# Hybrid decoder block on one core: sums of squares of queries by four products in column groups of TensorE, and the norms of row blocks in one chain

## The chip, the cores and the metric

One NeuronCore of a Trainium2 chip runs the whole kernel in one launch. The metric is the time on the device in microseconds, the median over runs. Engines are named as in the profile: PE is TensorE's matmul unit and PEld its weight load, DVE is VectorE, ACT ScalarE, POOL GpSimd, SP SyncE, whose queue issues every transfer of this kernel.

## The reference

For x of 1024 rows and 1024 columns (float32) the layer computes two branches from one projection, merges them, and adds an MLP:

```python
h = rms_norm(x, norm_mix_g); proj = h @ w_in
gq, gk, gv = split(silu(causal_short_conv(g_qkv, conv_w)))          # 8 heads of 128
gq = l2_normalize(gq) * 128 ** -0.5; gk = l2_normalize(gk)
o_gdn = rms_norm(gated_delta_rule_chunked(gq, gk, gv, g, beta), gdn_norm_g) * silu(z)
o_att = dsa_sparse_attention(a_q, a_k, a_v, i_q, i_k, i_w)          # top 256 keys per query
x = x + (sigmoid(gate_a) * o_gdn + sigmoid(gate_b) * o_att) @ w_out
h2 = rms_norm(x, norm_mlp_g)
x = x + square(relu(h2 @ w_mlp_up)) @ w_mlp_down
```

l2_normalize divides a query by the root of its sum of squares plus 1e-6, and rms_norm of the second kind divides a row of the new x by the root of the mean of its squares. The change is about these two sums.

## The kernel before

The kernel is one stream of instructions per engine, whose order is fixed when it is built. The order comes from a planner, the class Weave (L2092): each piece of work is a generator with a priority (a smaller number goes first), which yields when it wants others to have a turn, when it waits for a named event, or, by yielding "A", "V" or "G", until that engine is free. Weave keeps a clock, prices each instruction by simple formulas (L2202 to L2223), and always takes the ready generator of the best priority. On the chip each engine then runs its list strictly in that order and waits on semaphores.

The stages, in the order of time: input norm and first projections (to about 250 us); the gated-delta branch, head after head, beside dense products of 512 columns with weights in a high and a low part (gdense, to about 940); sparse attention in 16 steps (8 blocks of 128 rows, in the order 0, 7, 1, 6, 2, 3, 5, 4, and two groups of heads; values_out turns the softmax rows pr into pt on PE) with the output projection; from about 1140 the MLP, whose two products are computed by a scheme of seven products of halves, so that sums and differences of row blocks (t1 to t4) are turned, rounded to a high and a low part, and multiplied.

*Queries.* conv (L774) makes q of a head as 128 channels by 1024 positions. queries (L1015) first calls squares (L918): PE transposes the eight blocks of q into two banks of the ring tt, and ACT squares each block with an accumulated sum over the channels, which gives qss, one number per position with positions on partitions. Then come the products of keys and queries. The only reader of qss is output (L1114), after the scan of the head.

*Norms of row blocks.* residual (L1413) adds the output projection to a block x1, stores it to XD, and has ACT sum its squares into nss. roots (L1439) turns such sums into reciprocal roots nr by 11 small DVE operations. norm2 (L1448) is started when the attention is nearly over: roots of blocks 0, 1 and 2, then of 3, scaling of both halves of each block (DVE the first, ACT the second), transposes, and rounding in norm_out. early (L1481), once for blocks 6 and 7 and once for block 5, takes roots, scales the second half on ACT, and forms sums and differences; early_columns (L1499) turns them and early_rounded (L1525, priority 2) rounds them, ACT the high part hh and DVE the low part hl, and frees the bank. norm2b (L1677, priority -1) does the same for block 4, the last; its last_columns (L1704) needs a bank of the ring ss. Behind the event ("T", 2, 3) it subtracts t4[j] -= t2[j] for all four blocks in one go.

Of the kernel before, what the change touches and what calls it, by code (L numbers as in the profile page):

```python
# [9 lines left out]
F32 = mybir.dt.float32  # L10
F32R = mybir.dt.float32r
BF16 = mybir.dt.bfloat16
# [14 lines left out]
H = 8  # L27
# [23 lines left out]
def body(tc, a, out, dbg=None):  # L51
# [26 lines left out]


    padl, padl_es = pool("padl", side="left")  # L80
    G.memset(padl.tile([P, 32], F32, name="padl"), 0.0)
    cst, cst_es = pool("cst", side="left")
    dr, dr_es = pool("dr", space=DRAM)
    htp, ht_es = pool("htp", side="left")
# [110 lines left out]
    def after(key):  # L195
        wv.add(0, later(wv.busy["SY"] + SY_LATENCY, key))
# [478 lines left out]

    M1 = [dr.tile([4, P, S], F32, name=f"M1_{g}") for g in range(2)]
    SG = [dr.tile([4, P, S], F32, name=f"SG_{g}") for g in range(2)]
    ZA = [dr.tile([NB, 4, 32, 32], F32, name=f"ZA{h}") for h in range(H)]
    ZU = [dr.tile([NB * 4, 8, 4, 32], F32, name=f"ZU{h}") for h in range(H)]

# [93 lines left out]
    def conv(u):  # L774
        h, c = gunits[u]
        ct = ctile[c] + h
        yield ("gp",)
        if len(convs) > 1:
            yield ("conv", convs[-2])
        convs.append(u)  # L780
        cu = gq.tile([P, 3 + S], F32, name="cu", bufs=2)
        G_.memset(cu[:, 0:3], 0.0)
        for half in range(2):
            yield ("half", (u, half))
            wv.add(-1, cdrain(cu, u, half))
# [12 lines left out]
        yield  # L798
        o = (gq if c == "v" else gp).tile([P, S], F32, name={"k": "kt", "q": "qt", "v": "t4"}[c],
                                          bufs={"k": 3, "q": 2, "v": 1}[c])  # L800
        A_.activation(o, cu[:, 0:S], AF.Copy, scale=cw[0])
        for j in range(1, 4):
            yield
            yield "V"
            V_.scalar_tensor_tensor(o, cu[:, j:j + S], cw[j], o, op0=OP.mult, op1=OP.add)
        yield
        yield "A"
        A_.activation(cu[:, 0:S], o, AF.Tanh, scale=0.5)
        yield
        yield "V"  # L810
        V_.scalar_tensor_tensor(o, cu[:, 0:S], 1.0, o, op0=OP.add, op1=OP.mult)
        yield
        st[h][c + "t"] = o
        wv.done("conv", u)
        wv.add(2, {"k": keys, "q": queries, "v": values}[c](h))

# [98 lines left out]
        wv.add(1, join(h))  # L915


    def squares(t, ss):  # L918
        for half in range(2):
            yield tt.ready  # L920
            ps, slot_ = tt.get()
            for i in range(4):
                PE_.transpose(ps[:, i, :], blk(t, half * 4 + i), ident)
            yield
            for i in range(4):
                b = half * 4 + i
                junk = gp.tile([P, P], BF16, name="gj")
                A_.activation(junk, ps[:, i, :], AF.Square, accum_out=ss[:, b:b + 1])
                if i % 2:
                    yield  # L930
            tt.free(slot_)


    def decayed(h):
# [81 lines left out]
    def queries(h):  # L1016
        qt = st[h]["qt"]
        yield ("keys", h)
        if h > 1:
            yield ("out", h - 2)  # L1020
        kt, aq = st[h]["kt"], st[h]["aq"]
        qss = st[h]["qss"] = gp.tile([P, NB], F32, name="qss", bufs=3)
        yield from squares(qt, qss)
        for half in range(2):
            hs = slice(half * 4, half * 4 + 4)
            yield tt.ready
            ps, slot_ = tt.get()
# [85 lines left out]

    def output(h):  # L1114
        yield ("gate", (h, "a"))
        oss, qss, oo, og = (st[h][k] for k in ("oss", "qss", "vv", "kt"))
        fo = gp.tile([P, NB], F32, name="fo", bufs=2)
        fe = gp.tile([P, NB], F32, name="fe", bufs=2)
# [294 lines left out]
    def residual(qb, pw):  # L1413
        yield ("x", qb)
        yield 0.2
        for c in range(2):
            cs = slice(c * HALF, (c + 1) * HALF)
            V_.tensor_tensor(x1[qb][:, cs], x1[qb][:, cs], pw[c], op=OP.add)
        yield
        wv.done("x1", qb)  # L1420
        SY_.dma_start(XD[qb * P:(qb + 1) * P, :], x1[qb])
        after(("xd", qb))
        junk = tp.tile([P, D], BF16, name="th", bufs=2)
        A_.activation(junk, x1[qb], AF.Square, accum_out=nss[:, qb:qb + 1])
        yield
        wv.done("ss", qb)
# [9 lines left out]
        yield  # L1436
        wv.done("h2k", half, k)

    def roots(tbs):  # L1439
        for tb in tbs:  # L1440
            yield ("ss", tb)
        bs = slice(min(tbs), max(tbs) + 1)
        V_.tensor_scalar(nms[:, bs], nss[:, bs], 1.0 / D, EPS, op0=OP.mult, op1=OP.add)
        yield from rsq_w(cst, nr[:, bs], nms[:, bs], len(tbs), "n2", apart=False)
        yield


    def norm2():  # L1448
        tbs = [qb for qb, g in ATT if g and qb // 4 == first]
        for now in (tbs[:3], tbs[3:]):  # L1450
            yield from roots(now)
            for tb in now:
                yield ("xd", tb)
                for c, eng in enumerate("VA"):
                    yc = x1[tb][:, c * HALF:(c + 1) * HALF]
                    yield eng
                    if c:
                        A_.activation(yc, yc, AF.Copy, scale=nr[:, tb:tb + 1])
                    else:
                        V_.tensor_scalar(yc, yc, nr[:, tb:tb + 1], None, op0=OP.mult)  # L1460
        yield
        for c in range(2):
            ys = [x1[first * 4 + i][:, c * HALF:(c + 1) * HALF] for i in range(4)]
            for k in range(4 * c, 4 * c + 4):
# [13 lines left out]
    y22, comb, pairs = {}, {}, {}  # L1478
    places = {0: 0, 2: 2, 3: 4, 1: 6}

    def early(tbs):  # L1481
        yield from roots(tbs)
        for tb in tbs:
            i, r = tb % 4, nr[:, tb:tb + 1]
            b11, b12 = part(first, 0)[i], part(1 - first, 0)[i]
            y22[i] = part(1 - first, 1)[i]
            yield ("xd", tb)
            yield "A"
            A_.activation(y22[i], y22[i], AF.Copy, scale=r)
            yield  # L1490
            yield ("turned", 0)
            yield "V"
            V_.scalar_tensor_tensor(b11, b12, r, b11, op0=OP.mult, op1=OP.subtract)
            yield "V"
            V_.scalar_tensor_tensor(b12, b12, r, y22[i], op0=OP.mult, op1=OP.subtract)
            yield
            wv.done("combined", i)

    def early_columns():  # L1499
        js = [tb % 4 for tb in EARLIER]  # L1500
# [3 lines left out]
        for m in (0, 2):  # L1504
# [6 lines left out]
            for k in range(4):  # L1511
# [6 lines left out]
                ps, slot_ = ring.get()  # L1518
                for j in js:
                    PE_.transpose(ps[:, j * P:(j + 1) * P], y22[j][:, k * P:(k + 1) * P], ident)  # L1520
                wv.add(2, early_rounded(m, k, ps, ring, slot_))
        yield
        wv.done("early")

    def early_rounded(m, k, ps, ring, slot_):  # L1525
        cs = slice(min(EARLIER) % 4 * P, (max(EARLIER) % 4 + 1) * P)
# [25 lines left out]
    vl[1] = pA.tile([P, NB, P], F32R, name="vl1")  # L1552
    wv.add(1, vprep(1))
    wv.add(4, score())
    wv.add(0, loadm())
    wv.add(0, loadx())
    wv.add(1, wout_weights())
# [12 lines left out]

    wv.run(until=("pv", NA - 2))
    wv.add(8, norm2())
    for tbs in (EARLIER[1:], EARLIER[:1]):
        wv.add(2, early(tbs))
    wv.add(2, early_columns())


# [99 lines left out]
    def norm2b():  # L1677
# [15 lines left out]
        V_.scalar_tensor_tensor(t3[i], t3[i], r, y, op0=OP.mult, op1=OP.subtract)  # L1693
        yield ("T", 2, 3)
        wv.add(1, columns(3, t3))
        yield "V"
        for j in range(4):
            V_.tensor_tensor(t4[j], t4[j], t2[j], op=OP.subtract)
        yield ("col", 3)
        wv.add(1, columns(1, t1))  # L1700
        yield ("col", 1)
        wv.add(1, columns(4, t4))

    def last_columns(m, i, row):  # L1704
# [480 lines left out]
class _Ordered:  # L2185
# [12 lines left out]
    def __getattr__(self, op):  # L2198
# [3 lines left out]
        def call(*args, **kw):  # L2202
# [5 lines left out]
            if name == "PE":  # L2208
                fast = op == "matmul" and args[1].dtype == F32R
                if op == "matmul" and not fast and "tile_position" not in kw:  # L2210
                    return wv.issue(name, ins, (n * 1.67 + 5) / 1e3, 0.25)
                if op == "matmul" and "tile_position" in kw:
                    return wv.issue(name, ins, 0.03, 0.25)
                return wv.issue(name, ins, (n * (0.417 if fast else 0.835) + (13.4 if wv.shared else 2.5)) / 1e3, 0.25)
            if name == "SY":
                return wv.issue(name, ins, max(0.5, n * o.shape[0] / 9e4), SY_LATENCY)
            if name == "A":
                return wv.issue(name, ins, 0.13 + n / 1200 + (0.1 if "accum_out" in kw else 0), 0.15)
            if name == "V":
                return wv.issue(name, ins, 0.07 + n / 960, 0.12, self.port(op, args, kw))  # L2220
            if op == "tensor_tensor":
                return wv.issue(name, ins, 0.33 + n / 476, 0.2, True)
            return wv.issue(name, ins, 0.15 + n / 1000, 0.2)  # L2223
# [50 lines left out]
```

## Time and profile before

| | us |
|---|---|
| median of 3 runs | 1806.71 |
| lowest and highest run | 1806.06, 1808.27 |
| the profiled execution's own time | 1806.61 |
| its span, first to last instruction | 1804.9 |

The span is what the profile shows; the 1.7 us between it and the execution's own time lie around it. Durations are of instructions as the profiler records them; matmuls are pipelined, so that a row's start to the next row's start says more than its length. All operations are recorded by one helper, so every row has the same line, L2203, and tiles are told apart by their names: tt is the ring of banks for transposes of the gated-delta stage, dd the bank of dense products, jj that of the small products in tiles of the array, w a slot that holds weights or a row block, m a slot of the MLP.

### The profile page before, as it was taken

Reading aid. Unit: us, or ns where it says so; the run is one execution under the profiler, and the core shown is the slowest. Engines: PE = TensorE matmul, PEld = TensorE weight load, DVE = VectorE, ACT = ScalarE, POOL = GpSimd, SP = SyncE. Lnnn points to the kernel's source line nnn. Section 1 sums busy time; section 2 is a strip of 40 time slices with the busy share of each in tenths; the row PEclk is TensorE's granted clock in tenths of the full one; section 3 lists DMA queues with packets and bytes.
Section 4 is the critical chain, followed back from the end, with each engine's and each line's share of the span. In section 5 each row is a group of like instructions: output and inputs, shape, how many; then the busy total and the mean of one; then the engine's idle time right before and its main releaser. Section 6 shows DMA issues by size and latency. Waiting matters only on the chain.

```text
span 1804.9 us, 28444 instructions
## 1 busy us (share of the span) xinstructions
PE 1783.6 (99%) x10252; PEld 1517.6 (84%) x10252; DVE 1287.2 (71%) x2746; ACT 1022.8 (57%) x2186; POOL 533.3 (30%) x738
## 2 busy tenths in 40 slices
PE   9999999999999999999999999989999999999999
PEld 8999998888888888888888888768888888888887
DVE  5556768867877788875368677776766668969673
ACT  6566656656676554553457666666766664333331
POOL 0003530743362415753014121222323222222230
PEclk9999999999999999999999999999999999999999
DMA  5111242232222222232355221315445459473241
GB/s 165 50 47 47 71 129 65 50 97 77 66 64 71 53 65 69 75 86 75 95 186 183 76 90 53 114 38 184 167 152 170 135 185 363 133 250 122 100 136 52
DMA packets 192193, 198.80 MB, mean 110 GB/s; under 512 B 36738, under 2 KB 140467, under 8 KB 192051
## 3 DMA queue, kind: packets, MB, share of 16 engines
q1 hardware_dynamic: 192050, 196.97, 34.7%
q8 instruction: 81, 1.33, 0.3%
q14 instruction: 62, 0.50, 0.1%
HBM read 141.20 MB, written 55.74 MB: 109 GB/s over the span
## 4 chain that ended last, share of the span: by engine, by line
PE 93%; DVE 4%; ACT 1%; issue 1%; POOL 1%; DMA 0%; SPq 0%; ACTq 0%; POOLq 0%; DVEq 0%
PE dd L2203 55%; PE o L2203 15%; PE s L2203 7%; PE pt L2203 6%; PE tt L2203 3%; PE cc L2203 2%; PE sq L2203 2%; PE oo L2203 1%; PE jj L2203 1%; DVE w L2203 1%; DVE hl L2203 1%; DVE m L2203 0%; PE tp L2203 0%; DVE n2t L2203 0%; DMA pj<-in_x_dram 0%
## 5 line engine op out<-in xcount | busy, mean ns | idle before, releaser
L2203 PE MATMUL dd<-hh,w 128*128 128x512 f32 x1568 | 517.4, 401 | 0.0
L2203 PEld LDWEIGHTS dd<-hh,w 128*128 128x128 f32 x1568 | 289.0, 189 | 51.4
L2203 PE MATMUL dd<-hl,w 128*128 128x512 f32 x784 | 316.2, 403 | 0.9 <-DVE hl L2203 0.9
L2203 ACT ACTIVATE m<-m 128x512 f32<-128x512 f32 (+1 forms) x240 | 139.9, 625 | 79.3 <-PE dd L2203 34.3
L2203 PE MATMUL dd<-w,hh 128*128 128x256 f32 x960 | 179.4, 284 | 0.4 <-DVE w L2203 0.4
L2203 PE MATMUL dd<-hh,m 128*128 128x512 f32 x520 | 173.5, 398 | 0.7 <-DVE w L2203 0.5
L2203 DVE TENSOR_TENSOR m<-m,m 128x512 fp32r<-128x512 f32 (+2 forms) x184 | 143.3, 804 | 38.7 <-ACT m L2203 33.3
L2203 PEld LDWEIGHTS dd<-hl,w 128*128 128x128 f32 x784 | 147.8, 189 | 26.4 <-DVE hl L2203 1.4
L2203 PEld LDWEIGHTS dd<-w,hh 128*128 128x128 f32 x960 | 151.5, 191 | 1.5 <-DVE w L2203 0.6
L2203 PE MATMUL dd<-w,hl 128*128 128x256 f32 x480 | 136.2, 284 | 0.0
L2203 POOL TENSOR_TENSOR sx<-sx,stmp 128x60 f32<-128x60 f32 (+24 forms) x248 | 119.7, 483 | 19.4
L2203 PEld LDWEIGHTS dd<-hh,m 128*128 128x128 f32 x520 | 97.6, 190 | 20.4 <-DVE w L2203 2.0
L2203 POOL TENSOR_TENSOR stmp<-sx,um 128x60 f32<-128x60 f32 (+24 forms) x186 | 83.4, 448 | 89.5 <-DMA um<-ZA 61.8
L2203 POOL TENSOR_TENSOR m<-m,m 128x512 f32<-128x512 f32 x48 | 69.0, 1445 | 120.6 <-DVE m L2203 63.3
L2203 PE MATMUL dd<-hl,m 128*128 128x512 f32 x260 | 103.2, 397 | 0.9 <-POOL hl L2203 0.9
L2203 DVE TENSOR_SCALAR_CACHE_REDUCE tkeq<-sc,cand 128x384 f16<-128x384 f32 (+3 forms) x128 | 103.3, 807 | 1.0
L2203 ACT ACTIVATE hh<-m 128x1024 fp32r<-128x1024 f32 x44 | 45.1, 1056 | 90.0 <-PE s L2203 42.0
L2203 ACT ACTIVATE ha<-m 128x1024 fp32r<-128x1024 f32 x44 | 45.3, 1056 | 86.0 <-PE o L2203 34.9
L2203 PEld LDWEIGHTS dd<-w,hl 128*128 128x128 f32 x480 | 91.8, 191 | 0.6
L2203 DVE TENSOR_TENSOR w<-w,w 128x1024 fp32r<-128x1024 f32 (+1 forms) x63 | 71.0, 1130 | 22.5 <-ACT w L2203 21.7
L2203 ACT ACTIVATE tkcm<-sc,cand 128x896 f16<-128x896 f32 x64 | 70.0, 1094 | 28.3 <-DVE cand L2203 25.2
L2203 ACT ACTIVATE w<-w 128x1024 fp32r<-128x1024 f32 x48 | 50.8, 1058 | 53.9 <-PE dd L2203 53.7
(413 smaller groups left out, 4412.2 us busy)
## 6 DMA issues: line engine op xcount, KB each, us to landing
HD<-m SPq DMA_DIRECT2D x112, 256.0 KB, 2.3
m<-HD SPq DMA_DIRECT2D x56, 512.0 KB, 3.9
w<-in_w_in_dram SPq DMA_DIRECT2D x48, 512.0 KB, 4.0
m<-in_w_mlp_up_dram SPq DMA_DIRECT2D x33, 512.0 KB, 4.8
wraw<-in_w_in_dram SPq DMA_DIRECT2D x8, 1024.0 KB, 5.3
m<-in_w_mlp_down_dram SPq DMA_DIRECT2D x16, 512.0 KB, 7.4
w<-in_x_dram SPq DMA_DIRECT2D x10, 512.0 KB, 5.5
es<-GC SPq DMA_DIRECT2D x8, 512.0 KB, 4.9
```

Of the source, the lines that this page charges most:

```text
L2203: ins = f(*args, **kw)
```

## The change

The squares of q are taken by ACT over the whole 128 by 1024 tile, and summed over the channels by four products with a matrix of ones, 128 by 32, each with 256 positions and each at its own 32 columns of the array and 32 partitions of one bank. ACT copies the bank to SBUF; one row of each group goes to a new buffer QS in memory, and a transfer brings QS back with positions on partitions. This runs inside conv for q, before its event, and output waits for a new event ("qss", h). The tile of zeros padl becomes the tile of ones.

The roots of all row blocks but the last are done by one generator, norms, two blocks at a time in the order of the attention, the first two groups with a yield after each operation; it is started with the attention. scaled, one per block, scales as soon as the block is stored. norm2 and early only wait for it. early_rounded goes from priority 2 to 0, and the subtractions of t4 for blocks 5, 6 and 7 move from norm2b to the end of early_columns. residual's sums of squares no longer count the store's issue as a delay, and two of the planner's prices change.

```diff
-    G.memset(padl.tile([P, 32], F32, name="padl"), 0.0)
+    ones32 = padl.tile([P, 32], F32, name="padl")
+    G.memset(ones32, 1.0)
...
+    QS = dr.tile([H, S], F32, name="QS")
...
         st[h][c + "t"] = o
+        if c == "q":
+            yield from query_squares(h, o, cu[:, 0:S])
         wv.done("conv", u)
...
-    def squares(t, ss):
-        for half in range(2):
-            yield tt.ready
-            ps, slot_ = tt.get()
-            for i in range(4):
-                PE_.transpose(ps[:, i, :], blk(t, half * 4 + i), ident)
-            yield
-            for i in range(4):
-                b = half * 4 + i
-                junk = gp.tile([P, P], BF16, name="gj")
-                A_.activation(junk, ps[:, i, :], AF.Square, accum_out=ss[:, b:b + 1])
-                if i % 2:
-                    yield
-            tt.free(slot_)
+    def query_squares(h, o, sq):
+        yield "A"
+        A_.activation(sq, o, AF.Square)
+        yield
+        yield tt.ready
+        ps, slot_ = tt.get()
+        ps = ps.rearrange("p a b -> p (a b)")
+        for c in range(4):
+            PE_.matmul(ps[32 * c:32 * c + 32, 0:256], ones32, sq[:, 256 * c:256 * c + 256], start=True, stop=True,
+                       tile_position=(0, 32 * c))
+        yield
+        rows = tp.tile([P, HALF], F32, name="th", bufs=2)
+        A_.activation(rows[:, 0:256], ps[:, 0:256], AF.Copy)
+        tt.free(slot_)
+        yield
+        wv.add(2, query_columns(h, rows))
+
+    def query_columns(h, rows):
+        for c in range(4):
+            SY_.dma_start(QS[h:h + 1, 256 * c:256 * c + 256], rows[32 * c:32 * c + 1, 0:256])
+        yield
+        qss = st[h]["qss"] = gp.tile([P, NB], F32, name="qss", bufs=3)
+        SY_.dma_start(qss, QS[h].rearrange("(b p) -> p b", p=P))
+        yield
+        wv.done("qss", h)
...
-        qss = st[h]["qss"] = gp.tile([P, NB], F32, name="qss", bufs=3)
-        yield from squares(qt, qss)
...
         yield ("gate", (h, "a"))
+        yield ("qss", h)
...
+        t = wv.t
         SY_.dma_start(XD[qb * P:(qb + 1) * P, :], x1[qb])
         after(("xd", qb))
+        wv.t = t
...
-    def roots(tbs):
+    def roots(tbs, apart=False):
...
-        yield from rsq_w(cst, nr[:, bs], nms[:, bs], len(tbs), "n2", apart=False)
+        yield from rsq_w(cst, nr[:, bs], nms[:, bs], len(tbs), "n2", apart=apart)
...
+    def norms():
+        qbs = [qb for qb, g in ATT if g]
+        for n, grp in enumerate((qbs[0:2], qbs[2:4], qbs[4:6], qbs[6:7])):
+            yield from roots(sorted(grp), apart=n < 2)
+            for tb in grp:
+                wv.add(2, scaled(tb))
+
+    def scaled(tb):
+        yield ("xd", tb)
+        r = nr[:, tb:tb + 1]
+        for c, eng in enumerate("VA"):
+            yc = x1[tb][:, c * HALF:(c + 1) * HALF]
+            if eng == "A":
+                yield eng
+                A_.activation(yc, yc, AF.Copy, scale=r)
+            elif tb // 4 == first:
+                yield eng
+                V_.tensor_scalar(yc, yc, r, None, op0=OP.mult)
+        yield
+        wv.done("scaled", tb)
...
     def norm2():
-        tbs = [qb for qb, g in ATT if g and qb // 4 == first]
-        for now in (tbs[:3], tbs[3:]):
-            yield from roots(now)
...
+        for tb in range(first * 4, first * 4 + 4):
+            yield ("scaled", tb)
...
-    def early(tbs):
-        yield from roots(tbs)
-        for tb in tbs:
...
-            yield ("xd", tb)
-            yield "A"
-            A_.activation(y22[i], y22[i], AF.Copy, scale=r)
...
+    def early(tb):
...
+        yield ("scaled", tb)
+        yield ("turned", 0)
...
-                wv.add(2, early_rounded(m, k, ps, ring, slot_))
+                wv.add(0, early_rounded(m, k, ps, ring, slot_))
         yield
         wv.done("early")
+        for j in js:
+            yield ("turned", 1)
+            yield "V"
+            t4 = part(first, 1)[j]
+            V_.tensor_tensor(t4, t4, y22[j], op=OP.subtract)
+        yield
+        wv.done("early", 4)
...
     wv.add(4, score())
+    wv.add(2, norms())
...
-    for tbs in (EARLIER[1:], EARLIER[:1]):
-        wv.add(2, early(tbs))
+    for tb in EARLIER[::-1]:
+        wv.add(2, early(tb))
...
-        yield "V"
-        for j in range(4):
-            V_.tensor_tensor(t4[j], t4[j], t2[j], op=OP.subtract)
         yield ("col", 3)
         wv.add(1, columns(1, t1))
         yield ("col", 1)
+        yield ("early", 4)
+        yield "V"
+        V_.tensor_tensor(t4[i], t4[i], t2[i], op=OP.subtract)
+        yield
         wv.add(1, columns(4, t4))
...
-                    return wv.issue(name, ins, 0.03, 0.25)
+                    return wv.issue(name, ins, 0.03 if n <= 64 else 0.11, 0.25)
...
-                return wv.issue(name, ins, 0.07 + n / 960, 0.12, self.port(op, args, kw))
+                return wv.issue(name, ins, (0.17 if n < 16 and wv.shared else 0.07) + n / 960, 0.12, self.port(op, args, kw))
```

## Rows read from the trace of the kernel before

**Rows 1.** The page's first part: busy time of each engine in us, its share of the span, and the number of its instructions.

```profile
PE 1783.6 (99%) x10252; PEld 1517.6 (84%) x10252; DVE 1287.2 (71%) x2746; ACT 1022.8 (57%) x2186; POOL 533.3 (30%) x738
```

**Rows 2.** The stretches of the span, all engines: stretch and its length in us, busy time of each engine in it (with the number of instructions), the granted clock of TensorE as a share of full speed, the busy share of the DMA engines, GB/s.

```profile
200.00:900.00 700.00, 699.71 (x4619) 595.69 (x4619) 519.66 (x1387) 403.36 (x1054) 284.76 (x576) 1.00 0.28 74
900.00:1100.00 200.00, 198.52 (x1053) 166.02 (x1052) 144.36 (x413) 124.80 (x252) 43.49 (x32) 1.00 0.39 127
1100.00:1240.00 140.00, 130.37 (x657) 107.14 (x655) 100.36 (x231) 85.46 (x171) 28.54 (x21) 0.98 0.28 91
1240.00:1700.00 460.00, 459.99 (x2030) 380.69 (x2029) 347.15 (x409) 253.10 (x414) 128.87 (x73) 1.00 0.53 180
```

**Rows 3.** The waits of PE between 1100 and 1240 us: for whom, us in total, times, the longest.

```profile
PE s L2203 <- DVE hl L2203: 4.9, 3, 3.2
PE pt L2203 <- ACT pr L2203: 3.1, 1, 3.1
```

**Rows 4.** PE alone in the 4 us after each of the two long waits: stretch, length, busy time, granted clock, DMA share, GB/s.

```profile
1144.00:1148.00 4.00, 4.00 (x13) 0.57 0.00 0
1188.00:1192.00 4.00, 3.49 (x11) 0.57 0.15 57
```

**Rows 5.** Timeline of PE around the transposes of a query, head 0: start in us, us, engine, line, operation, out<-in, rows*columns of the array, moving tile, count.

```profile
307.01 0.60 PE L2203 MATMUL tt<-ident,qt 128*128 128x128 f32 x4
307.44 0.60 PE L2203 MATMUL tt<-ident,t 128*128 128x128 f32 x4
307.80 0.48 PE L2203 MATMUL dd<-hl,w 128*128 128x512 f32 x1
308.11 0.63 PE L2203 MATMUL dd<-hh,w 128*128 128x512 f32 x2
```

**Rows 6.** The instructions that write gj from tt, ACT's squares of the queries: count, ns of one (least, median, most), first and last start, shape.

```profile
L2203 ACT ACTIVATE gj<-tt x64: 254/277/296, 307.6 to 809.5; 128x128 bf16<-128x128 f32 x64
```

**Rows 7.** Timelines of SP and of ACT: a load of weights for a dense unit, and ACT's split of the same weights into a high and a low part (what is in brackets is ACT's idle time before it, and what ended it).

```profile
331.47 0.38 SPq L2203 DMA_DIRECT2D w<-in_w_in_dram  x1
...
337.62 1.06 ACT L2203 ACTIVATE w<-w 128x1024 fp32r<-128x1024 f32 x1 [4.62 <-PE dd L2203]
```

**Rows 8.** Timelines of PE around two bursts of small products in tiles of the array, in 32 by 32 tiles (16 products, two records each) and in 64 by 64 tiles (8 products).

```profile
369.40 0.39 PE L2203 MATMUL dd<-hl,w 128*128 128x512 f32 x1
369.71 0.45 PE L2203 MATMUL jj<-um,am 32*32 32x32 f32 x32
370.10 0.74 PE L2203 MATMUL dd<-hh,w 128*128 128x512 f32 x2
370.67 0.39 PE L2203 MATMUL dd<-hl,w 128*128 128x512 f32 x1
...
860.22 0.39 PE L2203 MATMUL dd<-hl,w 128*128 128x512 f32 x1
860.54 0.68 PE L2203 MATMUL jj<-um,am 64*64 64x64 f32 x16
861.15 0.73 PE L2203 MATMUL dd<-hh,w 128*128 128x512 f32 x2
861.72 0.40 PE L2203 MATMUL dd<-hl,w 128*128 128x512 f32 x1
```

**Rows 9.** Timeline of PE, four products of queries and keys (fp32, two records each) on the whole array, and what follows.

```profile
318.38 1.05 PE L2203 MATMUL tt<-qt,kt 128*128 128x128 f32 x8
319.19 0.48 PE L2203 MATMUL dd<-hl,w 128*128 128x512 f32 x1
319.51 0.60 PE L2203 MATMUL tt<-ident,kt 128*128 128x128 f32 x4
```

**Rows 10.** The page's issues of transfers: out<-in, queue, operation and count, KB each, median us from issue to landing.

```profile
w<-in_w_in_dram SPq DMA_DIRECT2D x48, 512.0 KB, 4.0
...
ZU<-sx SPq DMA_DIRECT2D x32, 32.0 KB, 2.5
```

**Rows 11.** Timelines of DVE, ACT and PE around 1140 us, engine after engine.

```profile
1137.32 0.17 DVE L2203 TENSOR_SCALAR nms<-nss 128x2 f32<-128x2 f32 x1
...
1142.46 0.16 DVE L2203 RECIPROCAL mx<-nm 128x1 f32<-128x1 f32 x1
...
1138.49 0.19 ACT L2203 ACTIVATION_READ_ACCUMULATOR pr<-pr,nm 128x1 f32 x1
1140.53 0.72 ACT L2203 ACTIVATE w<-w,nr 128x512 f32<-128x512 f32 x1 [1.86 <-DVE nr L2203]
...
1143.54 0.84 PE L2203 MATMUL pt<-ident,pr 128*128 128x128 f32 x5 [3.11 <-ACT pr L2203]
```

**Rows 12.** The stores of the eight row blocks to XD on SP's queue: ns of one (least, median, most), first and last start in us.

```profile
L2203 SPq DMA_DIRECT2D XD<-w x8: 327/336/497, 977.4 to 1175.7; - x8
```

**Rows 13.** Timelines of PE, ACT and DVE around 1185 us, and of DVE at 1201.

```profile
1181.02 0.49 PE L2203 MATMUL s<-ident,w 128*128 128x128 f32 x3
...
1188.51 1.09 PE L2203 MATMUL s<-ident,hh 128*128 128x128 f32 x4 [3.24 <-DVE hl L2203]
...
1184.71 0.86 ACT L2203 ACTIVATE hh<-s 128x384 fp32r<-128x384 f32 x2
...
1187.82 0.55 DVE L2203 TENSOR_TENSOR hl<-s,hh 128x384 fp32r<-128x384 f32 x1
...
1201.75 3.46 DVE L2203 TENSOR_TENSOR w<-w,w 128x512 f32<-128x512 f32 x4
```

More of the change, by code (lines that the diff above doesn't have):

```diff
@@ L1437, in norm_out @@
         wv.done("h2k", half, k)
-    def roots(tbs):
+    def roots(tbs, apart=False):
         for tb in tbs:
             yield ("ss", tb)
-        bs = slice(min(tbs), max(tbs) + 1)
+        bs = slice(tbs[0], tbs[-1] + 1, max(1, tbs[-1] - tbs[0]))
         V_.tensor_scalar(nms[:, bs], nss[:, bs], 1.0 / D, EPS, op0=OP.mult, op1=OP.add)
-        yield from rsq_w(cst, nr[:, bs], nms[:, bs], len(tbs), "n2", apart=False)
+        yield from rsq_w(cst, nr[:, bs], nms[:, bs], len(tbs), "n2", apart=apart)
         yield
-    def norm2():
-        tbs = [qb for qb, g in ATT if g and qb // 4 == first]
-        for now in (tbs[:3], tbs[3:]):
-            yield from roots(now)
-            for tb in now:
-                yield ("xd", tb)
[L1454 to L1461, printed above, removed]
+    def norms():
[17 more added lines that the diff above has]
+        wv.done("scaled", tb)
+    def norm2():
+        for tb in range(first * 4, first * 4 + 4):
+            yield ("scaled", tb)
         for c in range(2):
@@ L1479, in body @@
     places = {0: 0, 2: 2, 3: 4, 1: 6}
-    def early(tbs):
-        yield from roots(tbs)
-        for tb in tbs:
[L1484 to L1487, printed above, removed]
-            yield "A"
-            A_.activation(y22[i], y22[i], AF.Copy, scale=r)
-            yield
-            yield ("turned", 0)
-            yield "V"
[L1493 to L1497, printed above, removed]
+    def early(tb):
+        i, r = tb % 4, nr[:, tb:tb + 1]
+        b11, b12 = part(first, 0)[i], part(1 - first, 0)[i]
+        y22[i] = part(1 - first, 1)[i]
+        yield ("scaled", tb)
+        yield ("turned", 0)
+        yield "V"
+        V_.scalar_tensor_tensor(b11, b12, r, b11, op0=OP.mult, op1=OP.subtract)
+        yield "V"
+        V_.scalar_tensor_tensor(b12, b12, r, y22[i], op0=OP.mult, op1=OP.subtract)
+        yield
+        wv.done("combined", i)
     def early_columns():
@@ L1520, in early_columns @@
                     PE_.transpose(ps[:, j * P:(j + 1) * P], y22[j][:, k * P:(k + 1) * P], ident)
-                wv.add(2, early_rounded(m, k, ps, ring, slot_))
+                wv.add(0, early_rounded(m, k, ps, ring, slot_))
         yield
         wv.done("early")
+        for j in js:
+            yield ("turned", 1)
+            yield "V"
+            t4 = part(first, 1)[j]
+            V_.tensor_tensor(t4, t4, y22[j], op=OP.subtract)
+        yield
+        wv.done("early", 4)
     def early_rounded(m, k, ps, ring, slot_):
@@ L1695, in norm2b @@
         wv.add(1, columns(3, t3))
-        yield "V"
-        for j in range(4):
-            V_.tensor_tensor(t4[j], t4[j], t2[j], op=OP.subtract)
         yield ("col", 3)
@@ L1701, in norm2b @@
         yield ("col", 1)
+        yield ("early", 4)
+        yield "V"
+        V_.tensor_tensor(t4[i], t4[i], t2[i], op=OP.subtract)
+        yield
         wv.add(1, columns(4, t4))
```

## The prediction

> **What bounds the kernel.** I read the views in the order in which they narrow the place. The busy times come first: TensorE 1783.6 us, 99% of the span, VectorE next with 71% [rows 1]. So an edit counts only by what TensorE has to do, by the time it waits, or by its clock. The stretches come second [rows 2]. In 200 to 900, where the squares of the queries lie, TensorE is busy 699.71 of 700 us: work taken off it there is a gain in full, and no wait is there to be won. In 1100 to 1240, where the norms of the row blocks feed the MLP, it is busy 130.37 of 140 at a granted clock of 0.98. From 1240 to 1700 it is busy 459.99 of 460, so what is won before 1240 arrives at the end undiminished. The waits come third: of the 9.6 us that TensorE stands idle in 1100 to 1240, 3.1 are for ScalarE's pr in one piece and 4.9 in three pieces, the longest 3.2, for VectorE's hl [rows 3]. After the two long ones the granted clock averages 0.57 over 4 us, between the levels 1.2 and 2.4 GHz, which costs 4 x 0.43 = 1.7 us each [rows 4]. That stretch thus holds 9.6 + 3.4 = 13.0 us, the most that the second half of the change can win.
>
> **The change, part by part.** The sum is made against the profiled execution's own time, 1806.6 us; the median of the three runs, 1806.71, is 0.1 above it.
>
> *Squares, taken away.* Per head 8 transposes. Eight of them (4 of qt, 4 of vt) start at 307.01 and the second product behind them at 308.11; one product of 512 columns lies in between, at 0.23 (459.99 us over 2030 products [rows 2]). That leaves 0.87 us [rows 5], so 8 heads give back 7.0 us. ScalarE loses 64 squares of 0.28 [rows 6] with their readings, and gains per head one pass over 1024 columns (1.06 for another of that size [rows 7]) and a copy of 256. Both lie beside a full TensorE and cost or win nothing. If that cover went, the three new steps (square, products, copy; about 3 us) would hold q's conv longer, whose buffer is wanted two units later, a unit being 48 x 0.23 = 11 us of TensorE.
>
> *Squares, added.* Per head four fp32 products of 256 columns, each at its own 32 columns of the array. Their price has two parts. The first is leaving the full array and coming back. Around the tiled burst at 369.71, three 512-column products take from 369.40 to 370.67, 1.27 instead of 0.69, so the burst costs 0.58; its starts spread over 0.45 - 0.19 = 0.26. The burst at 860.54 costs 1.50 - 0.69 = 0.81, spread 0.68 - 0.22 = 0.46 (0.19 and 0.22 are what one such record takes) [rows 8]. The rest, 0.32 and 0.35, is the price of the two switches; I take 0.33. The second part is the work. An untiled fp32 product is two records, and eight records of 128 columns take 1.13 - 0.23 = 0.90 us, 0.11 each [rows 9]; at 256 columns a product costs 0.45 us. The trace has no tiles of 128 rows and 32 columns. In its nearest rows, 8 products of 64 columns would need 0.9 in turn and spread over 0.46, on two column groups that share their rows; 16 products of 32 columns, on four tiles, spread over 0.26 instead of 0.9 [rows 8]. Column groups therefore overlap, and I take 0.45 for all four at once. The ends: 0.23, if a tile runs a product's two records together, and 1.80, one after another. With 0.33 + 0.45 = 0.78 against 0.87, eight heads win 0.7 us (between a gain of 2.5 and a loss of 10.1). This half of the change is all but neutral: the switches eat what the columns save.
>
> *Rows turned through memory.* Per head five transfers on SP's queue: four rows of 1 KB out, and one read that lays 1024 single numbers across partitions. The read waits on SP for the writes, and the weight loads stand behind it. Nearest rows: 32 KB in short pieces land in 2.5 us, a load of weights in 4.0 [rows 10]. I take 2.5 for the wait and up to 4 for the read. A weight load with little room was issued at 331.47 and its split began at 337.62, 2.1 us after a landing of 4.0 [rows 7]; behind the split TensorE still has most of a unit of 11 us. So 6 us of delay are hidden, and one beyond some 10 us per head would show. output(h) now waits for the numbers too, but stands behind the whole scan. Cost 0, with the strict bound that a delay of 15 would cost 5 per head.
>
> *The wait at 1140.* VectorE runs the roots of two row groups in one piece from 1137.32 to 1142.5, 22 small operations; the reciprocal that a softmax row needs stands behind them at 1142.46 although the sum was read by 1138.7, and TensorE resumes at 1143.54 [rows 11]. In the new order the groups (0,7) and (1,6) are done as their blocks arrive (eight blocks between 977 and 1176 [rows 12]), one operation at a time; only group (2,3) falls here, 11 operations, half of the 5.2 us. The reciprocal moves up by 2.5, which leaves 0.6 of 3.1. I let the clock stay up then, as it does through the 1.5 us of waits in 900 to 1100 [rows 2]. Gain 2.5 + 1.7 = 4.2.
>
> *The wait at 1185.* The transposes of 1181.02 are rounded by ScalarE only at 1184.71 and by VectorE only at 1187.82; the last block's transposes need that bank and start at 1188.51 [rows 13]. The change lifts this rounding from priority 2 to 0 and takes the scaling of blocks (0.72 each on ScalarE [rows 11]) out of this stretch. Against it, three of the four subtractions of t4 (3.46 us for the four [rows 13]) move to this place. What is late next is the last block's own roots on VectorE. I leave 1.0 of 3.2 and let the clock stay up: gain 2.2 + 1.7 = 3.9, between 0 and 4.9.
>
> *The small waits,* 4.9 - 3.2 = 1.7 for hl [rows 3] and 1.6 of others: the four subtractions at 1201.75 stood ahead of hl [rows 13], and one stays. I take 1.3 of 3.3.
>
> *What is moved in.* Five blocks' scaling and two root groups now run between 977 and 1137 [rows 11, 12]. Some of it will make a softmax row late: 1.5 us, between 0 and 14.4 (three waits of the 1140 kind, 3.1 + 1.7 each). The planner's new prices, and a block's chain that no longer waits out its store, only change orders; they are in these bounds at 0.
>
> Sum: 1806.6 - 0.7 - 4.2 - 3.9 - 1.3 + 1.5 = **1798.0 us**.
>
> **Rivals.** *Records in strict order.* If the second record of a product, which needs the tile of the first, holds back the next product, the four overlap only pairwise: 5 x 0.225 = 1.13 us instead of 0.45. Eight heads lose 5.4: 1803.4. For it: the burst on two column groups fits that as well. Against it: 16 products on four tiles would take 0.45 that way and took 0.26, though there the rows differ too [rows 8]. Chance 0.18. The Trainium skill (TensorE: Matmul & The Clock Gate, Part 3: Packing small matmuls) has matmuls start and end strictly in program order, which would make the time that of this rival; the rows of this case leave it open.
> *No overlap at all:* 1.80 instead of 0.45, 10.8 us more, 1808.8. The bursts of rows 8 speak against it. Chance 0.07.
> *The second wait stays,* since its chain starts from the last block and not from the order: 1798.0 + 3.9 = 1801.9. Chance 0.10.
> *The waits only change place,* the norms being late in another order: about 1806. Chance 0.05.
> *Slower:* the scalings and roots moved into the attention stage stand in ScalarE's and VectorE's queues ahead of a softmax row, and TensorE waits for pr as it does at 1140, with the clock falling, 4.8 us each. From three such waits on, the 8.6 won are more than spent: 1798.0 + 14.4 = 1812.4. For it: that is how the present 3.1 us came about, and there are seven new places. Against it: in 900 to 1100 VectorE is busy 144 of 200 and ScalarE 125 [rows 2]. Chance 0.15.
>
> **The numbers.** The forecast has 0.45; its own range is 1792.5 to 1802. A measurement of this kernel tells about 0.2%, 3.6 us, from no change, so faster means under 1803.0. Faster: 0.45, half of the strict order (which lies on the border), 0.10 of the second wait, 0.64 in all. Same: the other half, 0.07 and 0.05, 0.21. Slower: 0.15. The range from 1792.5 (most of the 13.0 won, the squares at 2.5) to 1809 (no overlap) leaves out the slower rival and the tails.
>
> **What would show it.** Right: eight tiled records per head, with the next full products about 0.8 us late in all; no transposes of qt; TensorE still full in 200 to 900; waits for pr and hl under 1 us, and the clock at full share from 1100 to 1240. The forecast is wrong if such a burst costs over 1.2 us, if TensorE waits over 3 us between 977 and 1137, or if a wait over 3 us stays near 1185.

## The result and the profile after

The changed kernel takes 1795.37 us (median of 5 runs, 1794.4 to 1795.79); the kernel before took 1807.31 beside it. The ratio is 0.9932, with a 95% interval from 0.992 to 0.9943: 11.9 us faster, where 8.6 was forecast (1798.0 from 1806.6). The profiled execution took 1795.37 us, its span is 1793.7, so that 1.7 us lie around the span, as before.

The page's first part for the changed kernel, to be read against [rows 1]: TensorE does the same number of products in 3.5 us less of busy time, and the span is 11.2 shorter. (The medians differ by 11.9, the two profiled executions, 1806.61 and 1795.37, by 11.2.)

```profile
PE 1780.1 (99%) x10252; PEld 1509.9 (84%) x10252; DVE 1286.3 (72%) x2746; ACT 1011.3 (56%) x2074; POOL 540.7 (30%) x738
```

The stretches of the changed kernel, with the columns of [rows 2]:

```profile
200.00:900.00 700.00, 699.30 (x4620) 589.91 (x4620) 522.76 (x1394) 392.12 (x941) 291.87 (x576) 1.00 0.28 74
900.00:1100.00 200.00, 198.51 (x1046) 165.21 (x1045) 146.03 (x433) 125.63 (x253) 44.67 (x33) 1.00 0.41 132
1100.00:1240.00 140.00, 138.77 (x719) 115.49 (x718) 107.50 (x224) 94.92 (x195) 35.25 (x25) 1.00 0.28 92
1240.00:1700.00 460.00, 459.83 (x2029) 380.53 (x2029) 338.60 (x399) 246.48 (x395) 124.14 (x70) 1.00 0.53 180
```

The reader is to look at the third row. TensorE is busy 138.77 of 140 us instead of 130.37, 8.4 more, and the granted clock is 1.00 instead of 0.98. The two dips of 0.57 cost 3.4 us before [rows 4], so this one stretch gives 8.4 + 3.4 = 11.8 us. In the other three rows TensorE is busy 0.6 us less in all (0.41, 0.01 and 0.16), which leaves the 11.2 of the span. All that the view of PE's waits lists in that stretch (for whom, us in total, times, the longest), against the 4.9 and 3.1 us of [rows 3]:

```profile
PE s L2234 <- DVE la L2234: 1.1, 1, 1.1
```

(la, like hl and pl, is the low part of a split tile, written by DVE.) PE after that wait and at the place of the old wait near 1185, with the busy times of all engines; the clock (third figure from the right), 0.57 in [rows 4], stays at its upper level, 2.4 GHz:

```profile
1145.00:1149.00 4.00, 3.68 (x24) 2.92 (x25) 3.81 (x7) 2.56 (x6) 0.00 (x0) 1.00 0.00 0
1188.00:1192.00 4.00, 4.00 (x19) 3.19 (x17) 4.00 (x5) 2.10 (x4) 2.44 (x3) 1.00 0.18 68
```

**The squares.** Timeline of PE around the new products of head 0, to be read against [rows 5, 8]:

```profile
291.51 0.39 PE L2234 MATMUL dd<-hl,w 128*128 128x512 f32 x1
291.74 0.61 PE L2234 MATMUL dd<-hh,w 128*128 128x512 f32 x2
292.29 0.64 PE L2234 MATMUL tt<-cu,padl 128*32 128x256 f32 x8
292.86 0.50 PE L2234 MATMUL dd<-hl,w 128*128 128x512 f32 x1
293.19 0.62 PE L2234 MATMUL dd<-hh,w 128*128 128x512 f32 x2
```

From 291.51 to 293.19 are 1.68 us, with four products of 512 columns in them at 0.227; what is left, 0.77, is the price of the burst. The eight transposes took 0.87. SP's queue for the same head: four writes and the read back, with a gap of under 1 us between them.

```profile
293.40 1.13 SPq L2234 DMA_DIRECT2D QS<-th  x4
295.46 0.38 SPq L2234 DMA_DIRECT2D qss<-QS  x1
```

**The norms.** DVE near 1135, to be read against [rows 11]; the one group of roots that still falls here (two blocks), and the reciprocal of a softmax row behind it:

```profile
1134.49 0.17 DVE L2234 TENSOR_SCALAR nms<-nss 128x2 f32<-128x2 f32 x1
...
1136.46 0.16 DVE L2234 SCALAR_TENSOR_TENSOR nr<-n2t,nr 128x2 f32<-128x2 f32 x1
1136.54 0.16 DVE L2234 RECIPROCAL mx<-nm 128x1 f32<-128x1 f32 x1
```

PE, ACT and DVE around the rounding of blocks 5, 6 and 7, engine after engine, to be read against [rows 13]:

```profile
1172.23 0.49 PE L2234 MATMUL s<-ident,w 128*128 128x128 f32 x3
...
1182.09 0.63 PE L2234 MATMUL s<-ident,hh 128*128 128x128 f32 x4
...
1173.61 0.47 ACT L2234 ACTIVATE hh<-s 128x384 fp32r<-128x384 f32 x1
...
1177.35 0.55 DVE L2234 TENSOR_TENSOR hl<-s,hh 128x384 fp32r<-128x384 f32 x1
```

These transposes start 8.8 us earlier than before (1181.02), and ACT rounds 1.4 us after them instead of 3.7. The last block's transposes at 1182.09 have no bracket: PE did not wait for them.

### The profile page after: what moved, and what is told of

It is laid out like the page before. It is cut to its first block, busy times and chain, and to the rows that moved or that the text cites. A ratio compares the mean times of both kernels' runs of the same rounds, so it can differ in the third digit from the quotient of the medians.

```text
span 1793.7 us, 28398 instructions
## 1 busy us (share of the span) xinstructions
PE 1780.1 (99%) x10252; PEld 1509.9 (84%) x10252; DVE 1286.3 (72%) x2746; ACT 1011.3 (56%) x2074; POOL 540.7 (30%) x738
## 5 line engine op out<-in xcount | busy, mean ns | idle before, releaser
L2234 ACT ACTIVATE m<-m 128x512 fp32r<-128x512 f32 (+1 forms) x240 | 139.8, 625 | 78.7 <-PE o L2234 30.0
L2234 POOL TENSOR_TENSOR sx<-sx,stmp 128x60 f32<-128x60 f32 (+24 forms) x248 | 123.6, 498 | 19.4
L2234 POOL TENSOR_TENSOR stmp<-sx,um 128x60 f32<-128x60 f32 (+24 forms) x186 | 89.1, 479 | 100.3 <-DMA um<-ZA 86.5
L2234 ACT ACTIVATE tkcm<-sc,cand 128x896 f16<-128x896 f32 (+1 forms) x64 | 69.9, 1092 | 25.4 <-DVE cand L2234 21.8
L2234 PE MATMUL o<-hh,m 128*128 128x512 f32 x248 | 79.6, 389 | 0.0
```

What stands on the lines that cost most here:

```text
L2234: ins = f(*args, **kw)
```

## Experiments

All are compared with runs of the kernel before on the same chip. "Early" means that the norms start with the attention, "split" that the roots yield after each small operation.

| kernel | us | ratio to before, 95% |
|---|---|---|
| before, with the new squares only | 1807.45 | 1.0001 [0.9992, 1.001] |
| changed, with the old squares | 1795.66 | 0.9935 [0.9922, 0.9948] |
| changed, products in one column group | 1805.44 | 0.9988 [0.9979, 0.9997] |
| changed, products issued twice | 1810.15 | 1.0013 [1.0003, 1.0022] |
| changed, norms late and whole | 1802.73 | 0.9974 [0.9964, 0.9984] |
| changed, norms early and whole | 1807.09 | 0.9996 [0.9988, 1.0005] |
| changed, norms late and split | 1805.92 | 0.9989 [0.998, 0.9998] |
| before, split only | 1818.06 | 1.0056 [1.0044, 1.0069] |
| changed, all groups split | 1796.57 | 0.9937 [0.9925, 0.995] |
| changed, old price | 1795.15 | 0.9931 [0.9919, 0.9944] |
| changed, rounding at priority 2 | 1796.82 | 0.994 [0.9927, 0.9952] |
| changed, t4 in one go | 1796.84 | 0.9939 [0.9927, 0.9952] |

### Which half carries the gain

The kernel before with the squares of the change and nothing else of it but the price of a tiled product:

```diff
+        if c == "q":
+            yield from query_squares(h, o, cu[:, 0:S])
...
-        yield from squares(qt, qss)
```

> The kernel before with only the new squares of queries and their way through memory; norms as before. Theory: the four products overlap, a burst costs 0.77 us against 0.88 for eight transposes, so 0.9 us less in all and the long waits near 1140 and 1185 stay: ratio to before 0.9995, 1805.5 to 1807. Rival, that the squares bring a good part of the gain (by freeing ScalarE and the ring of banks in the gated-delta stage): over 3 us less, under 1804. Rival, that the new steps hold q's conv and cost: over 1808.

And the changed kernel with that half undone (squares in queries, no QS, no wait in output):

> The changed kernel with the old squares of queries (eight transposes, eight squares with sums); the norms chain and all else as changed. Theory: it has all of the gain but 0.9 us, ratio to before 0.9937, about 1796.3. Rival, that the squares bring over 3 us: 1798.5 or more.

Measured: 1.0001 and 0.9935. The squares win nothing that can be measured; the whole gain comes from the norms. The long waits of the first kernel in 1100 to 1240 are those of [rows 3], to a tenth:

```profile
PE s L2218 <- DVE hl L2218: 4.9, 3, 3.2
PE pt L2218 <- ACT pr L2218: 3.2, 1, 3.2
```

### Do the column groups overlap

All four products in one group (the copy and the writes behind them then read that group alone):

```diff
-            PE_.matmul(ps[32 * c:32 * c + 32, 0:256], ones32, sq[:, 256 * c:256 * c + 256], start=True, stop=True,
-                       tile_position=(0, 32 * c))
+            PE_.matmul(ps[0:32, 256 * (c % 2):256 * (c % 2) + 256], ones32, sq[:, 256 * c:256 * c + 256], start=True,
+                       stop=True, tile_position=(0, 0))
...
```

> The changed kernel with all four products of a head at the first 32 columns of the array instead of one in each group; the sums of half of the positions are overwritten and lost, the rest of the work is as changed. Theory, that column groups overlap: without them the work is four times 0.43, so a burst costs 0.77 + 1.29 = 2.1 us and eight heads lose 10.3, about 1805.7. Rival, that the records of a burst overlap by themselves and not by groups: within 1 us of 1795.4. Records start about 0.11 or 0.22 us apart instead of in two fours.

The four products issued twice:

```diff
-        for c in range(4):
+        for c in (0, 1, 2, 3, 0, 1, 2, 3):
```

> The changed kernel, with the four products of the sums of squares issued twice per head (the second time they write the same sums over the first). It separates the switch from the work: if the burst of 0.77 us is 0.29 to 0.33 for the two switches and 0.44 to 0.48 for the two rounds of records, it grows to about 1.25, +3.8 us in all, 1799.2. Rival: the work is only the spread of the starts, 0.26, and the switch 0.5: 1.03 per burst, +2.1, 1797.5. If eight products in column groups fall into strict turns, the burst grows by over 1.1.

Timelines of PE, head 0, first of the kernel with one column group:

```profile
292.24 0.39 PE L2234 MATMUL dd<-hl,w 128*128 128x512 f32 x1
292.46 0.61 PE L2234 MATMUL dd<-hh,w 128*128 128x512 f32 x2
293.01 1.91 PE L2234 MATMUL tt<-cu,padl 128*32 128x256 f32 x8
294.85 0.50 PE L2234 MATMUL dd<-hl,w 128*128 128x512 f32 x1
295.19 0.62 PE L2234 MATMUL dd<-hh,w 128*128 128x512 f32 x2
```

and then of the kernel with the products issued twice:

```profile
292.08 0.39 PE L2234 MATMUL dd<-hl,w 128*128 128x512 f32 x1
292.31 0.61 PE L2234 MATMUL dd<-hh,w 128*128 128x512 f32 x2
292.85 1.07 PE L2234 MATMUL tt<-cu,padl 128*32 128x256 f32 x16
293.85 0.50 PE L2234 MATMUL dd<-hl,w 128*128 128x512 f32 x1
294.19 0.64 PE L2234 MATMUL dd<-hh,w 128*128 128x512 f32 x2
```

Reckoned as above, the bursts cost 2.95 - 0.91 = 2.04 and 2.11 - 0.91 = 1.20 us. In one group the eight records follow one another, and the kernel loses 10.1 us, as expected. Issued twice, the burst grows by 0.43 to 0.44, the work of four products; the switches keep 0.33. The total of that kernel missed: 1810.15 instead of 1799.2. Its longer bursts explain some 3.5, and 6.5 lie where the attention begins: PE is busy 192.01 of 200 us in 900 to 1100 instead of 198.51, in another order of the planner's. Of the 14.8 us by which its median is longer, 4.8 stay unexplained. The burst settles the dispute; the total says nothing about it.

### Early or late, split or whole

The changed kernel with norms() started beside norm2, where the old one was, and roots in one piece (the edit of the roots stands last here, first in the file):

```diff
-    wv.add(2, norms())
...
+    wv.add(2, norms())
     wv.add(8, norm2())
...
-            yield from roots(sorted(grp), apart=n < 2)
+            yield from roots(sorted(grp), apart=False)
```

> The changed kernel with the chain of norms started where it stood before, with the transposes of the first half when the attention is nearly over, and each group of roots in one piece; priorities, subtractions and prices as changed. Theory: the wait for pr near 1140 comes back because the roots of six blocks stand in VectorE's queue ahead of a reciprocal: 3 to 5 us of wait and 1.7 of clock, ratio to the changed kernel about 1.003, near 1800. The wait near 1185 stays away. Rival, that the new prices and the priority alone removed that wait: within 1 us of 1795.4.

With the second edit alone:

> The changed kernel, with the norms started with the attention but every group's roots issued in one piece (11 small VectorE operations, about 2.6 us); nothing is left out. Theory: the early start is the cause of the gain at 1140, so this stays near 1795.4 with waits under 1 us each in 900 to 1140. Rival: a piece of 2.6 us on VectorE makes a softmax row late each time it falls badly; two of the four groups lie in the attention, each with a wait of 1 to 3 us: 1797.4 to 1802, and nearly the whole loss of the kernel with the late norms (1802.7) would then be due to the pieces and not to the start.

With the first alone:

> The changed kernel with the norms started at the old place, near the end of the attention, but with the first two groups' roots still split; nothing is left out. With the kernel of late and whole roots (1802.7) and that of early and whole ones (1807.1) it fills the square of start and pieces. If the pieces carry the gain: 1795.4 to 1797. If both are needed: near 1802.7. If it is only a matter of which order the planner falls into, neither: anything from 1796 to 1807, with its waits at other engines' work than in any of the three.

Early and split take 1795.4; each of the other three lies 7 to 12 us above. So in the changed kernel neither the start nor the pieces carry the gain by themselves, and my expectation that the early start would do was wrong. The waits of PE in 1100 to 1240, first with late and whole norms:

```profile
PE o L2234 <- DVE pl L2234: 2.2, 1, 2.2
PE s L2234 <- DVE hl L2234: 1.2, 1, 1.2
PE s L2234 <- DVE w L2234: 1.2, 1, 1.2
PE pt L2234 <- DVE la L2234: 1.2, 1, 1.2
```

with late and split norms:

```profile
PE pt L2234 <- DVE la L2234: 3.3, 1, 3.3
PE s L2234 <- DVE la L2234: 1.6, 1, 1.6
PE s L2234 <- DVE hl L2234: 1.4, 1, 1.4
PE dd L2234 <- DVE hl L2234: 1.2, 1, 1.2
```

and with early and whole ones:

```profile
PE dd L2234 <- DVE w L2234: 3.2, 2, 2.0
PE s L2234 <- issue: 2.3, 1, 2.3
PE dd L2234 <- DVE m L2234: 1.9, 1, 1.9
PE s L2234 <- DVE hl L2234: 1.7, 1, 1.7
```

The wait for pr, which I expected back in the first, is gone from all three, yet time is lost, mostly behind other VectorE work. The idle time of PE in 1100 to 1240 is 7.2, 8.0 and 9.9 us, against 1.2 in the changed kernel, and the clock falls in each: 0.91 in 1140 to 1160 with late and whole norms, 0.83 in 1160 to 1180 and 0.91 in 1200 to 1220 with late and split ones, 0.91 in 1160 to 1180 with early and whole ones. What is idle beyond 1.2, and the clock, come to about 7.8, 12 and 10.5 us, near the losses of 7.4, 10.6 and 11.7. Why these waits stand where they do is not shown; that late norms make something else late with them is my reading. What a whole piece does in the attention shows at once in the kernel of the last fence. DVE, the first group's roots and the row of maxima behind them:

```profile
1008.44 0.19 DVE L2234 TENSOR_SCALAR nms<-nss 128x2 f32<-128x2 f32 x1 [0.56 <-ACT th L2234]
...
1010.44 0.16 DVE L2234 SCALAR_TENSOR_TENSOR nr<-n2t,nr 128x2 f32<-128x2 f32 x1
1010.52 0.68 DVE L2234 CUSTOM_DVE_ANT_0 pr<-s,mk 128x512 f32<-128x512 f32 x1
```

and PE, whose next product waits for that row:

```profile
1011.26 0.50 PE L2234 MATMUL s<-kTh,qh 128*128 128x512 f32 x1 [1.10 <-DVE mx L2234]
```

That is a wait of 1.1; the other 10 us come later. In that kernel the fifth and the sixth row block are stored late (SP's queue):

```profile
1107.28 0.46 SPq L2234 DMA_DIRECT2D XD<-w  x1
...
1140.77 0.49 SPq L2234 DMA_DIRECT2D XD<-w  x1
```

In the changed kernel the same stores:

```profile
1097.82 0.50 SPq L2234 DMA_DIRECT2D XD<-w  x1
...
1133.87 0.45 SPq L2234 DMA_DIRECT2D XD<-w  x1
```

The blocks are 7 to 9.5 us later, so their norms, scalings and transposes start late. That the pieces alone put the blocks there isn't shown: with other durations of the planned work its order differs in many places at once. Nor do these stores alone tell a fast kernel from a slow one: the kernel before has them at 1105.0 and 1138.5, and both kernels with late norms at 1097.6 to 1097.9 and 1133.4 to 1133.8, like the changed one.

### The kernel before, split only

```diff
-        yield from rsq_w(cst, nr[:, bs], nms[:, bs], len(tbs), "n2", apart=False)
+        yield from rsq_w(cst, nr[:, bs], nms[:, bs], len(tbs), f"n2{tbs[0]}", apart=True)
```

> The kernel before with one edit: the roots yield after each small operation, so that other VectorE work can be planned between them (each group has its own scratch tile for it); start, priorities and subtractions as before, nothing is left out. It tells whether the splitting alone carries the gain. Theory of pieces: the wait for pr at 1140 goes (3.1 + 1.7 of clock), the one near 1185 stays: about 1802. Rival, order: no single edit carries it, because the planner makes another order of the attention's end with each, and the kernel with whole roots but the early start lost everything through such an order (1807.1): 1805 to 1809, with waits elsewhere.

Both expected totals missed. The kernel is slower by 10.2 us (1807.85 beside it), but not by waits: the one for pr is gone, and so is the long one near 1185. Of those for hl this is the longest that is left in 1100 to 1240, beside one of 0.7:

```profile
PE s L2203 <- DVE hl L2203: 1.3, 1, 1.3
```

The stretch itself, to be read against the third row of [rows 2]:

```profile
1100.00:1240.00 140.00, 136.70 (x700) 111.66 (x699) 106.51 (x254) 87.76 (x175) 29.07 (x22) 0.99 0.25 82
```

So with the splitting alone, at the old place, the wait at 1140 is gone, and TensorE is busy 136.70 us here instead of 130.37. Over the whole span it stands idle 15.7 us instead of 21.3. The time went elsewhere: its busy time is 1801.6 us instead of 1783.6. One stretch of the MLP, all engines, before and then in this kernel, and a later one of this kernel:

```profile
1300.00:1400.00 100.00, 100.00 (x443) 82.84 (x442) 64.96 (x94) 68.38 (x134) 33.12 (x23) 1.00 0.45 153
```

```profile
1300.00:1400.00 100.00, 100.00 (x432) 80.92 (x431) 64.11 (x95) 66.98 (x129) 29.02 (x20) 1.00 0.44 146
1600.00:1700.00 100.00, 100.00 (x442) 82.79 (x442) 78.44 (x69) 37.12 (x37) 24.36 (x9) 1.00 0.52 174
```

In 1300 to 1400 PE is full at the full clock in both, with 432 products instead of 443: 0.2315 us each instead of 0.2257. The dense stage has it too (4576 instead of 4619 in 200 to 900), but the end of the MLP does not: 442 products in 1600 to 1700, where the kernel before has 443. No other kernel here shows it. What this one does alone is to give each group of roots its own scratch tile, which should move the tiles that are placed behind it in SBUF; the trace shows no addresses, and I did not try the tiles without the splitting. The total of this run can therefore not be used for the theory. Its waits can, with a caution: they say that in the kernel before the pieces alone might have won most of what the change won, unless the waits went only because a slower TensorE leaves the others more time. The run doesn't separate the two.

### The small parts

```diff
-                wv.add(0, early_rounded(m, k, ps, ring, slot_))
+                wv.add(2, early_rounded(m, k, ps, ring, slot_))
```

> The changed kernel, with the rounding of blocks 5, 6 and 7 (early_rounded) back at priority 2; nothing is left out. Theory: the wait near 1185 went because this rounding moved ahead in ScalarE's and VectorE's orders. Then a wait for hl of about 3 us comes back before the last block's transposes, with a lowered clock behind it: 1795.4 + 3.2 + 1.7 = about 1800. Rival: the wait went because the scalings and subtractions left that stretch, and the priority counts for nothing: 1795.4, no wait over 1 us.

The rival was right about the wait near 1185, which stays away, though not about the total: 1796.82. Of the 1.4 us, 1.0 is a new wait later on, in 1240 to 1300, of o for ScalarE's m.

The subtractions of t4 in one go, after ("T", 2, 3):

```diff
-        for j in js:
-            yield ("turned", 1)
-            yield "V"
-            t4 = part(first, 1)[j]
-            V_.tensor_tensor(t4, t4, y22[j], op=OP.subtract)
-        yield
-        wv.done("early", 4)
...
+        yield "V"
+        for j in range(4):
+            V_.tensor_tensor(t4[j], t4[j], t2[j], op=OP.subtract)
...
-        yield ("early", 4)
-        yield "V"
-        V_.tensor_tensor(t4[i], t4[i], t2[i], op=OP.subtract)
-        yield
```

> The changed kernel, with the four subtractions of t4 in one go after the event (T, 2, 3), as before; nothing is left out. Theory: they cost the small waits alone, 3.5 us of VectorE ahead of hl where TensorE has a bank or two in hand: a wait of 1 to 1.5 us near 1200, about 1796.7. Rival: splitting them is what emptied VectorE near 1185, or they hide behind full TensorE: 1795.4 either way, with no wait near 1200.

Measured 1796.84; at 1200 PE waits for hl, at the place expected and somewhat shorter than the 1 to 1.5 us:

```profile
PE pt L2226 <- DVE hl L2226: 0.8, 1, 0.8
```

The roots of all groups split (apart=True):

> The changed kernel with the roots of all four groups split, not of the first two only; nothing is left out. If splitting is good as such, the 1.1 us wait of TensorE at 1145, behind the whole roots of the third group and what they pushed back on VectorE, shrinks: 1794.3 to 1795.4. If the choice of two groups was one order among many, some loss: 1796 to 1804, with new waits in 1100 to 1240.

Measured 1796.57: the wait for la at 1145 shrinks to 0.4, and one of 1.0 for a sum of a row block takes its place, with 1.4 us more of idle time in 1240 to 1700. The planner's old price (0.07 for every VectorE operation):

> The changed kernel, with the planner's old price for VectorE operations of under 16 columns (0.07 us instead of 0.17; the trace has 0.16 for a lone one and 0.195 from one start to the next in a chain). No instruction is added or taken away. If the price matters, the planner believes the roots shorter than they are, places them where they make something late, and 1 to 4 us come back: 1796.5 to 1799.5, with a wait of PE in 900 to 1240 behind a VectorE operation. If it does not: 1795.4.

Measured 1795.15, with an interval that covers the changed kernel's: the price is worth nothing that can be measured. No version beat the changed kernel by more than that. What the scaling of a block as soon as it is stored does by itself, and the store that no longer counts as a delay, was not tried.

## Why the forecast held

**Squares.** Forecast 0.78 per burst, 0.33 of it for the switches and 0.45 for the work; measured 0.77, 0.33 and 0.44. The gain of 0.7 for eight heads can't be seen outside the bursts. TensorE's busy time is 0.7 us less with the squares alone than before (1782.9 and 1783.6), but only 0.1 less in the changed kernel than with the old squares in it (1780.1 and 1780.2); a wait of 0.6 of tt for am came with the change; and the last product of the dense stage starts not earlier but 1.4 and 0.4 us later in these two pairs. The rivals *strict order* (1.13 for the work) and *no overlap* (1.80) fall: the four groups cost 0.44, and the same products in one group 2.04 - 0.33 = 1.71. That the four groups overlap was thus right. The time that I drew from the Trainium skill (TensorE: Matmul & The Clock Gate, Part 3: Packing small matmuls) for its rule of strict order is thus refuted here. The rule itself is not: the eight records start one after another, in two fours (6 to 8 ns apart in a four, 0.24 us from four to four), and the trace doesn't say which product each belongs to.

**Queue.** Forecast at no cost, with a wait of 2.5 us on SP. SP waited for the writes 6.4 us in 13 waits, 1.0 at most, and the squares alone measure 1.0001.

**The waits** are the terms that were too small, in sum 7.9 instead of 11.9 net. At 1140 I took 4.2 and all 4.8 went. Near 1185 I took 3.9 and all 4.9 went. Of the small ones I took 1.3 of 3.3 and nearly all went. Against that, moved-in work was to cost 1.5, and one wait of 1.1 for la at 1145 came. 4.8 + 4.9 + 3.3 - 1.1 = 11.9, which the stretch shows as 8.4 + 3.4. The forecast held, but the errors in the waits lie all on one side: each gain was priced too low.

**The reasons behind them** were right in part. That the reciprocal moves up is in the rows, and in the kernel before with the split alone that wait is gone. For the wait near 1185 I named the priority first: that was wrong, it stays away without it. What remains of my reasons is that the scalings left this stretch: ACT and DVE reach the rounding sooner, and the transposes themselves come 8.8 us earlier. How much of it each does, no run separates.

**The rival with the wrong chance** is *the waits only change place*. I gave it 0.05 at about 1806. Three kernels with the same edits but another start or other pieces ended there or on the way to it (1805.9, 1807.1 and 1802.7), each without the long waits of [rows 3] and with new ones for pl, la, w or m. I priced the waits one by one, and in this kernel their parts hold only together. *Slower*, with waits in the attention, did not occur: in 977 to 1137 the view lists no wait of PE in the changed kernel. Its mechanism is real, though: whole roots made one of 1.1 there.

Is the gain then one lucky order? Seven kernels keep early and split norms and change something else (old squares, one column group, products twice, price, priority, t4, all groups split). In all seven TensorE is busy 138.0 to 138.8 of 140 us in 1100 to 1240, at a granted clock of 1.00. Five of them take 1795.2 to 1796.8; the other two have longer bursts, and the one with the products issued twice shows that an order can still lose elsewhere. Six of the seven have the wait of 1.1 for la too, so their orders there are probably near the changed kernel's: the gain holds over these, and no more is shown.

## What to carry to other kernels

When a planner or a list scheduler sets the order, the removal of a wait is not yet a gain: with the norms late or in one block the two long waits went too, and others for VectorE's work took their place. So parts of such a change are to be tested together as well as alone, and by the total. Four thin products side by side in column groups cost one product's time (0.44 us) and a fixed switch (0.33); against the 0.87 of eight transposes that was nothing to measure, and I would expect it to pay only where the switch is spread over more work. After any edit look at the spacing of the products in a stretch that is full, before explaining a total by waits.

## Not expected of the hardware

- Full-array products of 512 columns ran at 0.2315 us on average instead of 0.2257 in 1300 to 1500, and the dense stage was slower too, with PE full and the clock at 1.00, in the one kernel with more scratch tiles. In 1600 to 1700 they ran as before. TensorE's busy time is 18 us longer in that kernel. Why is open.
- One record of 256 columns on 32 columns of the array takes the time of four beside each other: bursts of eight records in one group spread over 1.91 us, in four groups over 0.64, and sixteen in four groups over 1.07.
